# Emitting the output product of finished row blocks along with the sparse heads

## Chip, core and metric

The kernel runs on one core of one Trainium2 chip. The metric is the device time of one execution in microseconds (us), as a median over runs; for the kernel before it is 2643.86 us over 3 runs (2642.41 to 2647.59).

## What is computed

One layer of a hybrid attention encoder, for 2048 prompt rows and for a "sample" of 8 x 16 new rows with caches. One input projection feeds three groups of eight heads of 64 columns; each group's result is multiplied by a gate, and one output product ends the layer:

```python
def _merge(x, oa, ob, oc, p, w_out):
    g = jnp.concatenate([oa * jax.nn.silu(p['za']),      # A: causal, forget gate
                         ob * jax.nn.silu(p['zb']),      # B: 256 selected keys per row
                         oc * jax.nn.silu(p['zc'])], axis=-1)   # C: band of 9 chunks
    return x + jnp.einsum('bne,ed->bnd', g, w_out)       # 1536 -> 1024
...
y_prompt = _rmsnorm(hp, final_g)                         # same for y_sample
```

A row of the output thus needs all 24 heads of that row, and nothing of other rows.

## The kernel before

The 2048 prompt rows are 16 blocks of 128; block 16 is the sample. Products are made of float16 halves, so one logical product is three matmuls.

**Dense heads (A and C).** `attn_a` and `attn_c` return units of work, one for a head and a chunk of 512 queries. `chain` walks through the units: the row maxima of up to `LEAD` = 2 units run ahead of the unit whose weighted sum is being made. Each step of `chain` is emitted at high priority (`first`).

**Sparse heads (B).** `b_units` gives 32 units, two for each block of rows (four heads each), in the order of `ORDER`, block 15 first, block 0 last. A unit of block i has i + 1 steps, 272 steps in all. A step multiplies queries and keys into a `st` tile (three matmuls of 512 columns: with `KaB`, `K1B` and the mask `ng`), takes the exponential on ACT (`Pf`), its remainder `Pl` on POOL or DVE (L250), and adds twelve matmuls of 64 or 65 columns into `o` with `VB`. The maxima read `s` tiles (DVE, `jk`, L1236). A unit ends with `rs`, `u` (DVE, L1267 and L1269), `u` times the gate (POOL, L1270) and `gh` (ACT and DVE, L1272). After the second unit of a block SP issues a transposing transfer `gb<-gh` (L1275) and two writes `gTd<-gb` (L1277) into the scratch tensor `gTd` in HBM.

**The sample** (`sample_stream`, tiles `pj`, `acc`, `yy`, `rl`, `qi`) is spread over the steps 560 to 850 of `chain`, also at high priority; it writes block 16 of `gTd` (`gTd<-yy`).

**Output product.** `out_product` comes after all of this in the code. It opens the pool `ob` in the space of the dense heads' pool `aw`, loads and splits the weights `wo` (12 tiles of 128 x 1024), and for each block, `[16] + ORDER`, reads `gac<-gTd` (two transfers of 384 KB, one for each half), makes 2 x 36 matmuls of 512 columns into `pj`, adds the input row block `xr`, and normalises it: DVE L1402, ACT L1407, some 20 short DVE instructions, DVE L1413, then `out<-xr` on SP.

**What sets the order.** The code only sets priorities: a list scheduler places each engine's instructions by a timing model of its own, at high priority those of `chain` and of the sample, and fills in the others where it sees an engine free. On the chip each engine takes its list in that order.

Of the kernel before, what the change touches and what calls it, by code (L numbers as in the profile page):

```python
# [56 lines left out]
NV = 400  # L57
PITCH = 16 * 2 * NV - 1
# [4 lines left out]
def hybrid_step(ctx, tc, x_prompt, x_sample, cache_a_k, cache_a_v, cache_a_logf, cache_b_k, cache_b_v,  # L63
# [13 lines left out]
    def turn_t(out, in_):  # L77
        """blocks of 128 columns, transposed"""
        SP.dma_start_transpose(out.rearrange("p (j t) -> p j t", t=128), in_)
# [23 lines left out]
    # scratch  # L103
# [27 lines left out]
    # constants  # L131
# [110 lines left out]
    def exp_split(pool, st, lo, hi, bias):  # L242
        """P = exp: the upper halves of its words, and the rest"""
        Pf = pool.tile([128, 512], F32, name="Pf", bufs=PB)
        Pl = pool.tile([128, 512], F16, name="Pl", bufs=PB)
        Ph = Pf.bitcast(BF16).rearrange("p (n t) -> p n t", t=2)[:, :, 1]
        S.activation(Pf[:, lo:hi], st[:, lo:hi], AF.Exp, bias=bias, scale=1.0 / LOGIT)  # L247
        turn[0] += 1
        e = G if turn[0] % PD < (PN if nsl is None else PS) else V
        e.tensor_tensor(Pl[:, lo:hi], Pf[:, lo:hi], Ph[:, lo:hi], ALU.subtract)  # L250
        return Ph, Pl
# [19 lines left out]
    def finish(pool, O, hg, c):  # L271
        """gate one head of one chunk and lay it out for the output product"""
# [16 lines left out]
    def twice(e, r0, t0, n):  # L289
        """64 rows of queries, for both halves of the partitions"""  # L290
        a = qTd[e, r0:r0 + 64, t0:t0 + n]
        return bass.AP(tensor=a.tensor, offset=a.offset, ap=[[0, 2], [NT, 64], [1, n]])
# [9 lines left out]
    def vec(hh, f, off, ap):  # L302
        """rows of a table, each one element behind the row before"""
        base = rep[0, hh, f]
        return bass.AP(tensor=base.tensor, offset=base.offset + off, ap=ap)
# [5 lines left out]
    # normalised input, transposed and split  # L311
# [44 lines left out]
    def proj_t(wt, o, c, out):  # L356
        """out[col, token] for 128 columns at o"""
# [6 lines left out]
    def proj_n(wt, o, n, c, r, out, first):  # L364
        """out[token, col] for n columns at o of token block r of chunk c"""
# [90 lines left out]
    # the first chunks are projected while the next ones are normalised: forget gate, indexer, first keys and values  # L456
# [36 lines left out]
    # log sigmoid: min(x, 0) - 2 atanh((1 - T) / (3 + T)),  T = tanh(|x| / 2)  # L493
# [29 lines left out]
    # cumulative sum  # L523
# [36 lines left out]
    # position tables  # L560
# [25 lines left out]
    # indexer scores and the selected keys of one block of queries  # L586
# [25 lines left out]
    def select(i, out):  # L612
        """the 256 best keys of each row, ties to the lowest index: a threshold that 248..256 scores
        exceed, then the rest in order of value and index"""
# [49 lines left out]
        # a score equal to the threshold counts by half: take it off  # L664
# [35 lines left out]
    def select_plain(i, sl):  # L700
        """the same by 32 rounds of the eight largest"""
# [25 lines left out]
    def attn_a(h):  # L727
        """units of one head: the maxima of a chunk of queries, then its products"""
# [60 lines left out]
    def attn_c(h):  # L789
        """units of one head: the maxima of a chunk of queries, then its products"""  # L790
# [98 lines left out]
    # ------------------------------------------------------------------ the sample  # L889
    def sample_stream():  # L890
# [38 lines left out]
        def diag(t, outer):  # L929
            """the blocks on the diagonal of 8 x 8 blocks of 16 columns"""  # L930
# [116 lines left out]
        def gate_sums():  # L1047
            """forget-gate sums of the streams, relative to the end of the cache"""
# [107 lines left out]
    # ------------------------------------------------------------------ the selected keys  # L1156
    def b_units(kvp):
# [26 lines left out]
        def load_pair(c2):  # L1184
            """queries of two blocks"""
# [24 lines left out]
        def b1(u, x):  # L1210
            """the maxima of four heads"""
# [70 lines left out]
    # ------------------------------------------------------------------ order of the work  # L1282
# [7 lines left out]
    def chain(units):  # L1290
        """the maxima of the units, ahead of their products by LEAD units at most"""
        products = []
        done, k = 0, 0
        m = p = None
        while done < len(units):
            if m is None and k < len(units) and k <= done + LEAD:
                yield k
                x = []
                m = units[k][0](units[k][2], x)
                k += 1  # L1300
# [5 lines left out]
            if p is not None and next(p, END) is END:  # L1306
                p = None
                done += 1
            yield None

    def select_stream():
        """the scores of a block along with the selection of the block before"""
# [52 lines left out]
    def find_flag():  # L1365
        """rows whose threshold was not found"""
# [7 lines left out]
    def fill():  # L1374
        """projections, spread over the attention"""
# [4 lines left out]
    # ------------------------------------------------------------------ output product  # L1380
    def out_product():
        ob, ob_end = pool("ob", 2)
        wo = ob.tile([128, 2, 12, D], F16, name="wo", bufs=1)
        for k in range(12):
# [4 lines left out]
        fg = ob.tile([128, D], F32, name="fg", bufs=1)  # L1389
        SP.dma_start(fg, bass.AP(tensor=final_g.tensor, offset=final_g.offset, ap=[[0, 128], [1, D]]))  # L1390
        for b in [16] + ORDER:
            gac = ob.tile([128, 2, 12, 128], F16, name="gac")
            for e in range(2):
                SP.dma_start(gac[:, e], gTd[e, :, b * 128:(b + 1) * 128].rearrange("(k p) t -> p k t", p=128))
            xt = ob.tile([128, D], F32, name="xr")
            SP.dma_start(xt, xp[b * 128:(b + 1) * 128] if b < 16 else xs)
            for n in range(2):
                p = pj()
                seq = [(k, e, w) for k in range(12) for e, w in ((0, 0), (0, 1), (1, 0))]
                for q, (k, e, w) in enumerate(seq):  # L1400
                    mm(p, gac[:, e, k, :], wo[:, w, k, n * 512:(n + 1) * 512], start=q == 0, stop=q == len(seq) - 1)
                V.scalar_tensor_tensor(xt[:, n * 512:(n + 1) * 512], p, 1.0 / (HS * WS),  # L1402
                                       xt[:, n * 512:(n + 1) * 512], op0=ALU.mult, op1=ALU.add)
            ss = ob.tile([128, 2], F32, name="ss")
            for n in range(2):
                jk = ob.tile([128, 512], BF16, name="jk", bufs=1)
                S.activation(jk, xt[:, n * 512:(n + 1) * 512], AF.Square, accum_out=ss[:, n:n + 1])  # L1407
            ms = ob.tile([128, 1], F32, name="ms")
            V.tensor_tensor(ms, ss[:, 0:1], ss[:, 1:2], ALU.add)
            V.tensor_scalar(ms, ms, 1.0 / D, EPS, op0=ALU.mult, op1=ALU.add)  # L1410
            rr = ob.tile([128, 1], F32, name="rr")
            rsq(rr, ms, 1, ob, 1.0)
            V.scalar_tensor_tensor(xt, xt, rr, fg, op0=ALU.mult, op1=ALU.mult)  # L1413
            SP.dma_start(yp[b * 128:(b + 1) * 128] if b < 16 else ys, xt)
        ob_end.close()
# [5 lines left out]
    it = chain(units)  # L1421
# [7 lines left out]
    assert len(units) > na  # L1429
    while nsm is not None:  # L1430
        nsm += 1
        if first(smp_st) is END:
            nsm = None
    aw_end.close()
    out_product()
# [3 lines left out]
    # if a threshold was not found  # L1439
    with tc.If(fv > FORCE):  # L1440
# [4 lines left out]
        for _ in chain(b_units(None)):  # L1445
            pass
        out_product()
# [67 lines left out]
```

## Time and profile before

| | |
|---|---|
| median of 3 runs | 2643.86 us |
| span of the profiled execution | 2656.7 us |
| PE busy (matmuls) | 2393.3 us, 90% |
| DVE busy | 1866.7 us, 70% |
| ACT busy | 1368.9 us, 52% |
| POOL busy | 961.9 us, 36% |
| SP's hardware queue, share of 16 DMA engines | 40.1% |

The span runs from the first to the last instruction of the profiled execution; its own time outside the profiler is not given, and the span lies 12.8 us (0.5%) above the median of the runs. The busy time of an engine is averaged over all stages; the end of a matmul is modelled in the profile, so short waits of PE are under-counted.

### The profile page before, as it was taken

The numbers are of one execution on the slowest core, as the hardware profiler recorded it, in microseconds if no ns is written. First come the engines' busy times: TensorE is split into PE (matmuls) and PEld (weight loads), VectorE is DVE, ScalarE is ACT, GpSimd is POOL, SyncE is SP. The second block draws the span as 40 slices with busy tenths as digits, with TensorE's granted clock in tenths as the row PEclk, the third lists the DMA queues.
The fourth block names the chain that finished last, engine by engine and source line by source line (L and its number), as shares of the span: only waits on it lengthen the run. The fifth ranks groups of instructions, "written<-read, shape, count | busy, mean of one in ns | idle before, by whom it ended". The sixth has DMA issues, their size and how long they took to land.

```text
span 2656.7 us, 69205 instructions
## 1 busy us (share of the span) xinstructions
PE 2393.3 (90%) x26566; PEld 1654.3 (62%) x26566; DVE 1866.7 (70%) x5128; ACT 1368.9 (52%) x2725; POOL 961.9 (36%) x2241
## 2 busy tenths in 40 slices
PE   3898899999989989889999898879889999999998
PEld 2576567676766757666767666656656656555443
DVE  4334675877667766677677777888999988677433
ACT  5334464665547456465657465567666545433100
POOL 0013654344245243334333324535444454333000
PEclk9999999999999999999999999989999999999999
DMA  9747223343342323233333231664463322344542
GB/s 225 151 108 204 70 67 77 95 104 89 93 102 72 86 72 87 69 86 91 95 87 93 76 98 48 150 142 108 119 163 84 79 47 50 76 102 103 138 118 83
DMA packets 589286, 266.15 MB, mean 100 GB/s; under 512 B 412160, under 2 KB 577856, under 8 KB 588688
## 3 DMA queue, kind: packets, MB, share of 16 engines
q1 hardware_dynamic: 588944, 261.63, 40.1%
q8 instruction: 210, 3.44, 0.6%
q14 instruction: 132, 1.08, 0.1%
HBM read 160.37 MB, written 84.85 MB: 92 GB/s over the span
## 4 chain that ended last, share of the span: by engine, by line
PE 44%; DVE 16%; POOL 13%; DMA 11%; issue 9%; ACT 6%; SPq 1%; ACTq 0%; DVEq 0%; POOLq 0%
PE pj L72 27%; PE st L72 7%; PE o L72 4%; PE s L72 4%; ACT eq L637 2%; DMA wst<-in_w_in 2%; DVE jk L1236 2%; DVE Pl L250 2%; POOL ub L646 2%; DVE mx L759 1%; POOL eb L648 1%; DVE acc L607 1%; POOL eg L653 1%; DMA hT<-xh 1%; DMA rl<-out 1%
## 5 line engine op out<-in xcount | busy, mean ns | idle before, releaser
L72 PE MATMUL pj<-wt,hT 128*128 128x128 f16 (+1 forms) x8568 | 821.9, 244 | 2.0 <-DVE ev L82 1.0
L72 PEld LDWEIGHTS <-hT 128*128 128x128 f16 x8976 | 673.5, 99 | 210.9 <-DMA hT<-xh 50.6
L250 POOL TENSOR_TENSOR Pl<-Pf 128x512 f16<-128x512 f32 (+3 forms) x331 | 345.4, 1052 | 548.9 <-ACT Pf L247 473.6
L247 ACT ACTIVATE Pf<-st,sh 128x512 f32<-128x512 f32 (+1 forms) x496 | 295.4, 613 | 278.1 <-PE st L72 80.9
L72 PEld LDWEIGHTS <-Pf 128*128 128x128 bf16 x5472 | 326.1, 98 | 104.3 <-ACT Pf L247 20.5
L250 DVE TENSOR_TENSOR Pl<-Pf 128x512 f16<-128x512 f32 (+3 forms) x485 | 290.8, 606 | 102.7 <-ACT Pf L247 98.5
L72 PE MATMUL pj<-hT,wt 128*128 128x512 f16 (+1 forms) x1680 | 353.2, 355 | 1.2 <-DVE ev L82 1.0
L72 PEld LDWEIGHTS <-Pl 128*128 128x128 f16 x2736 | 258.8, 99 | 85.6 <-POOL Pl L250 30.4
L72 PE MATMUL pj<-wo,gac 128*128 128x512 f16 x1224 | 273.2, 380 | 3.4 <-DMA gac<-gTd 3.4
L72 PE MATMUL o<-V,Pf 128*128 128x65 f16 x3296 | 257.6, 195 | 13.8 <-ACT Pf L247 12.5
L637 ACT ACTIVATE eq<-acc,u 128x384 bf16<-128x384 f32 (+13 forms) x126 | 164.8, 1308 | 162.7 <-POOL u L660 159.1
L607 DVE SCALAR_TENSOR_TENSOR acc<-rl,iws,acc 128x512 f32<-128x512 f32 (+3 forms) x266 | 185.4, 697 | 89.8 <-ACT rl L601 86.6
L72 PEld LDWEIGHTS <-wt 128*128 128x128 f16 x1680 | 150.3, 99 | 148.6 <-issue 19.2
L72 PE MATMUL o<-V,Pl 128*128 128x65 f16 x1648 | 213.7, 194 | 29.0 <-POOL Pl L250 17.6
L247 ACT ACTIVATE Pf<-st,ncb 128x512 f32<-128x512 f32 (+1 forms) x320 | 191.3, 621 | 89.3 <-PE st L72 58.5
L1236 DVE CUSTOM_DVE_ANT_0 jk<-s,ng 128x512 bf16<-128x512 f32 (+3 forms) x304 | 187.2, 616 | 41.5 <-PE s L72 21.2
L759 DVE TENSOR_REDUCE mx<-s 128x1 f32<-128x512 f32 (+3 forms) x320 | 188.7, 602 | 33.5 <-PE s L72 32.5
L72 PEld LDWEIGHTS <-gac 128*128 128x128 f16 x1224 | 117.7, 98 | 141.1 <-DMA gac<-gTd 3.9
L601 ACT ACTIVATE rl<-s 128x512 f32<-128x512 f32 (+3 forms) x304 | 160.6, 540 | 85.4 <-PE s L72 70.4
L72 PE MATMUL st<-qp,Ka 128*128 128x512 f16 (+3 forms) x544 | 176.7, 330 | 13.9 <-ACT Pf L247 13.2
L72 PE MATMUL st<-Q,K 98*128 98x512 f16 (+3 forms) x544 | 172.8, 332 | 1.8 <-ACT Q L75 1.7
L72 PE MATMUL o<-VB,Pf 128*128 128x65 f16 (+1 forms) x2176 | 159.3, 194 | 1.1 <-ACT Pf L247 1.1
(473 smaller groups left out, 4465.3 us busy)
## 6 DMA issues: line engine op xcount, KB each, us to landing
wst<-in_w_in SPq DMA_DIRECT2D x84, 256.0 KB
gac<-gTd SPq DMA_DIRECT2D x34, 384.0 KB
out<-ev SPq DMA_DIRECT2D x96, 128.0 KB
qTd<-ev SPq DMA_DIRECT2D x96, 128.0 KB
szd<-ev SPq DMA_DIRECT2D x96, 128.0 KB
qp<-qTd SPq DMA_DIRECT2D x96, 128.0 KB
out<-xr SPq DMA_DIRECT2D x17, 512.0 KB
xt<-in_x_prompt SPq DMA_DIRECT2D x16, 512.0 KB
```

Of the source, the lines that this page charges most:

```text
L72: P.matmul(out, lhsT, rhs, start=start, stop=stop, skip_group_check=True)
L247: S.activation(Pf[:, lo:hi], st[:, lo:hi], AF.Exp, bias=bias, scale=1.0 / LOGIT)
L250: e.tensor_tensor(Pl[:, lo:hi], Pf[:, lo:hi], Ph[:, lo:hi], ALU.subtract)
L601: S.activation(r[:, :w], p[:, :w], AF.Relu)
L607: V.scalar_tensor_tensor(acc[:, k0:k0 + w], r[:, :w], iws[:, i, h:h + 1], acc[:, k0:k0 + w], op0=ALU.mult, op1=ALU.add, **kw)
L637: S.activation(jk[:, :n], x, AF.Sign, bias=b, accum_out=ss)
L646: G.tensor_scalar(ub, w, ub, None, op0=ALU.max)
L648: G.tensor_scalar(eb, a, eb, None, op0=ALU.max)
L653: G.tensor_tensor(g, e, ep, ALU.mult)
L759: V.reduce_max(mx[:, ii, kc:kc + 1], p[:, :w], axis=AX.X)
L1236: V.tensor_tensor_reduce(out=jk[:, :w], in0=p[:, :w], in1=ng[:, k0:k0 + w], scale=1.0, scalar=GONE, op0=ALU.add, op1=ALU.max, accum_out=mx ...
```

## The change

The output product becomes a generator that is started inside the loop over `chain`. As soon as the products of all dense units are emitted (`ndone[0] >= na`), the rest of the sample is emitted in one go, `aw` is closed and `ob` opened. From there on each step of the loop also emits one piece (`OUTN` = 1) of the output stream: one weight tile, or six of a block's matmuls. A prompt block may start when both its sparse units are done; the sample's block 16 is still first. What is left is emitted after the loop.

```diff
+    def out_block(ob, wo, fg, b):
...
+        for n in range(2):
+            p = pj()
+            seq = [(k, e, w) for k in range(12) for e, w in ((0, 0), (0, 1), (1, 0))]
+            for q, (k, e, w) in enumerate(seq):
+                mm(p, gac[:, e, k, :], wo[:, w, k, n * 512:(n + 1) * 512], start=q == 0, stop=q == len(seq) - 1)
+                if q % 6 == 5:
+                    yield
...
+    def out_stream(ob, wo, fg, ready):
+        yield from out_weights(ob, wo)
         for b in [16] + ORDER:
...
+            while b not in ready:
+                yield None
+            yield from out_block(ob, wo, fg, b)
...
+    it = chain(units, ndone)
+    out, ready = None, {16}
     while (v := first(it)) is not END:
...
-    assert len(units) > na
-    while nsm is not None:
-        nsm += 1
-        if first(smp_st) is END:
-            nsm = None
-    aw_end.close()
-    out_product()
+        if out is None and len(units) > na and ndone[0] >= na:
+            while nsm is not None:
+                nsm += 1
+                if first(smp_st) is END:
+                    nsm = None
+            aw_end.close()
+            ob, ob_end, wo, fg = out_open()
+            out = out_stream(ob, wo, fg, ready)
+        if out is not None:
+            for k in range(max(0, ndone[0] - na) // 2):
+                ready.add(ORDER[k])
+            for _ in range(OUTN):
+                next(out, END)
+    for k in ORDER:
+        ready.add(k)
+    for _ in out:
+        pass
+    ob_end.close()
```

Every engine has the same instructions as before; only their order differs, and only from the last dense heads on.

The first place is SP's list where the sample's last rows are written to `gTd` and block 16 is read back. `ng<-negd6` and `ng<-negd10` are the masks of sparse blocks 6 and 10, loaded shortly ahead of their units. Before:

```order
L1251 DMA sz_41607<-szd_65 128x4x64
L1152 DMA gTd_66<-yy_29338 64x4x128 x2
L1394 DMA gac_43990<-gTd_66 128x12x128
L1192 DMA qp1_42282<-qTd_63 64x4x256
L1204 DMA ng_41824<-negd6_75 128x896
L1193 DMA qp1_42282<-qTd_63 64x4x256
```

And after the change:

```order
L1153 DMA gTd_66<-yy_29338 64x4x128 x2
L1404 DMA gac_36475<-gTd_66 128x12x128
L1404 DMA gac_37145<-gTd_66 128x12x128
L1404 DMA gac_36475<-gTd_66 128x12x128
L1252 DMA sz_39797<-szd_65 128x4x64
L1404 DMA gac_37145<-gTd_66 128x12x128
L1193 DMA qp1_40969<-qTd_63 64x4x256
L1205 DMA ng_40205<-negd10_79 128x1408
```

The end of the sample and the start of the output product move from the place where the mask of sparse block 6 is loaded to that of block 10; block 15 (`gac_37145`) is read at the same place.

The second place is SP's list where sparse block 8 is finished: its transposing transfer, its writes, and what follows. Before (`gac_44218` is block 14):

```order
L1251 DMA sz_41832<-szd_65 128x4x64
L1275 DMA_TRANSPOSE gb_41598<-gh_40819 128x8x128
L1277 DMA gTd_66<-gb_41598 128x4x128 x2
L1251 DMA sz_42058<-szd_65 128x4x64
L1204 DMA ng_42286<-negd5_74 128x768
L1394 DMA gac_44218<-gTd_66 128x12x128 x2
```

After (`gac_42569` is block 8 itself):

```order
L1252 DMA sz_42882<-szd_65 128x4x64
L1276 DMA_TRANSPOSE gb_42565<-gh_41672 128x8x128
L1278 DMA gTd_66<-gb_42565 128x4x128 x2
L1404 DMA gac_42569<-gTd_66 128x12x128 x2
L1425 DMA out_0<-xr_41916 128x1024
L1252 DMA sz_43158<-szd_65 128x4x64
```

The block just written is now read back at once; before, the block read there had been written long ago. Blocks 7 to 4 follow the same pattern.

The third place is PE's list where the output product of block 8 begins after the change (`VB` belongs to the sparse unit that runs then):

```order
L73 MATMUL o_42595<-VB0_30623,Pf_42757 128x64
L73 LDWEIGHTS Pl_42758
L73 MATMUL o_42595<-VB0_30623,Pl_42758 128x65
L73 LDWEIGHTS gac_42569
L73 MATMUL pj_42575<-wo_36145,gac_42569 128x512
L73 LDWEIGHTS gac_42569
L73 MATMUL pj_42741<-wo_36145,gac_42569 128x512
```

Most matmuls of sparse block 7, and all of the lower blocks, stand behind these; before the change block 8 of the output product stood behind all sparse units.

Counted over PE's list: the sample's last matmul had 194 of the 272 sparse steps ahead of it before, and 102 after; of the 1224 matmuls of the output product 414 stood ahead of the last sparse matmul before, and 1026 after. The first matmul of the output product stands 290 rows (145 matmuls) behind the sample's last before, and 136 rows (68 matmuls) after. Between the last product of a block's second sparse unit and the first matmul of its output product stand, for blocks 8, 7, 6, 5 and 4, now 115, 123, 128, 96 and 152 matmuls, of which 16, 6, 37, 20 and 0 belong to the output product of other blocks; blocks 15 to 9 and 3 to 0 have more.

## Rows read from the trace of the kernel before

**Rows 1.** The page: the span, and busy time of the engines.

```profile
span 2656.7 us, 69205 instructions
...
PE 2393.3 (90%) x26566; PEld 1654.3 (62%) x26566; DVE 1866.7 (70%) x5128; ACT 1368.9 (52%) x2725; POOL 961.9 (36%) x2241
```

**Rows 2.** Busy time by stretch; the first numbers are the stretch and its length.

```profile
core 0: us, PE busy (x) PEld busy (x) DVE busy (x) ACT busy (x) POOL busy (x), PEclk, DMA share, GB/s
1690.00:1895.00 205.00, 170.03 (x2418) 121.58 (x2416) 179.19 (x483) 140.46 (x319) 99.36 (x108) 0.96 0.55 127
...
1942.00:2081.00 139.00, 127.96 (x1744) 85.81 (x1745) 131.66 (x385) 90.58 (x193) 64.22 (x64) 1.00 0.46 109
2081.00:2272.00 191.00, 180.53 (x2431) 120.98 (x2430) 169.09 (x506) 95.93 (x169) 95.94 (x102) 0.99 0.25 56
...
2281.00:2469.00 188.00, 187.04 (x1693) 102.26 (x1694) 135.24 (x439) 68.54 (x121) 59.12 (x61) 0.99 0.45 100
2469.00:2644.00 175.00, 174.95 (x815) 79.11 (x811) 65.43 (x268) 16.31 (x45) 0.73 (x1) 1.00 0.43 115
2644.00:2656.70 12.70, 0.00 (x0) 0.00 (x0) 5.15 (x23) 0.72 (x2) 0.00 (x0) 0.59 0.12 46
```

**Rows 3.** The chain that ended last, from 2268 to 2290: start, duration, what.

```profile
2271.16 3.71 DMA yy<-acc
...
2274.88 2.15 DMA gTd<-yy
...
2277.05 4.20 DMA gac<-gTd
...
2285.92 0.52 PE o L72 x17
```

**Rows 4.** PE's groups in 1942:2081, 2081:2272 and, last two, 2281:2469.

```profile
L72 PE MATMUL st<-Q2b,K1B 98*128 98x512 f16 x73 | 27.8, 380 | 0.0
...
L72 PE MATMUL st<-Q2b,K1B 98*128 98x512 f16 x103 | 39.2, 381 | 0.0
...
L72 PE MATMUL pj<-wo,gac 128*128 128x512 f16 x415 | 98.6, 381 | 3.4 <-DMA gac<-gTd 3.4
...
L72 PE MATMUL st<-Q2b,K1B 98*128 98x512 f16 x69 | 26.5, 384 | 0.0
```

**Rows 5.** The chain that ended last, from 1640 to the end.

```profile
1741.91 5.56 DMA rl<-in_cache_c_v
...
2469.13 174.84 PE pj L72 x810
...
2649.37 1.28 DVE xr L1413
```

**Rows 6.** PE's waits from 1690 to 2272: us, times, longest.

```profile
PE pj L968 <- ACT yy L75: 9.9, 6, 3.4
...
PE s L72 <- DVE mx L1236: 9.7, 21, 1.0
```

**Rows 7.** Timeline behind the last sparse unit's last product, and SP's part of it.

```profile
2468.90 0.10 PEld L72 LDWEIGHTS <-Pl 128*128 128x128 f16 x1
...
2469.94 0.73 POOL L1270 TENSOR_TENSOR u<-u,sz 128x256 f32<-128x256 f32 x1 [4.18 <-DVE u L1269]
...
2471.15 0.42 DVE L1272 TENSOR_TENSOR gh<-u,gh 128x256 f16<-128x256 f32 x1 [1.34 <-ACT gh L75]
2471.60 2.11 SPq L1275 DMA_TRANSPOSE gb<-gh  x1
...
2475.70 1.91 SPq L1277 DMA_DIRECT2D gTd<-gb  x2
```

**Rows 8.** Busy time by stretch around two waits of PE.

```profile
2178.80:2182.00 3.20, 0.34 (x2) 0.00 (x0) 1.22 (x4) 0.00 (x0) 1.91 (x2) 1.00 0.58 123
2182.00:2185.40 3.40, 3.28 (x39) 2.38 (x40) 3.40 (x11) 1.88 (x3) 0.00 (x0) 0.50 0.30 81
...
2281.00:2284.40 3.40, 3.11 (x17) 1.45 (x18) 1.14 (x3) 0.00 (x0) 0.00 (x0) 0.50 1.26 208
```

More of the change, by code (lines that the diff above doesn't have):

```diff
@@ L57 @@
 NV = 400
+OUTN = 1
 PITCH = 16 * 2 * NV - 1
@@ L1288, in first, with chain @@
             return next(g, END)
-    def chain(units):
+    ndone = [0]
+    def chain(units, done):
         products = []
-        done, k = 0, 0
+        k = 0
         m = p = None
-        while done < len(units):
-            if m is None and k < len(units) and k <= done + LEAD:
+        while done[0] < len(units):
+            if m is None and k < len(units) and k <= done[0] + LEAD:
                 yield k
@@ L1307, in chain @@
                 p = None
-                done += 1
+                done[0] += 1
             yield None
@@ L1378, in fill, with out_open, out_weights @@
             nfl = None if next(fil_st, END) is END else nfl + 1
-    def out_product():
+    def out_open():
         ob, ob_end = pool("ob", 2)
         wo = ob.tile([128, 2, 12, D], F16, name="wo", bufs=1)
+        fg = ob.tile([128, D], F32, name="fg", bufs=1)
+        SP.dma_start(fg, bass.AP(tensor=final_g.tensor, offset=final_g.offset, ap=[[0, 128], [1, D]]))
+        return ob, ob_end, wo, fg
+    def out_weights(ob, wo):
         for k in range(12):
@@ L1388, in out_product @@
             split_lo(wo[:, 1, k, :], wst, WS, wo[:, 0, k, :])
-        fg = ob.tile([128, D], F32, name="fg", bufs=1)
-        SP.dma_start(fg, bass.AP(tensor=final_g.tensor, offset=final_g.offset, ap=[[0, 128], [1, D]]))
-        for b in [16] + ORDER:
[L1392 to L1414, printed above, removed]
@@ L1415, in out_product @@
-        ob_end.close()
+            yield
+    def out_block(ob, wo, fg, b):
+        gac = ob.tile([128, 2, 12, 128], F16, name="gac")
+        for e in range(2):
+            SP.dma_start(gac[:, e], gTd[e, :, b * 128:(b + 1) * 128].rearrange("(k p) t -> p k t", p=128))
+        xt = ob.tile([128, D], F32, name="xr")
+        SP.dma_start(xt, xp[b * 128:(b + 1) * 128] if b < 16 else xs)
+        ss = ob.tile([128, 2], F32, name="ss")
+        for n in range(2):
[4 more added lines that the diff above has]
+                if q % 6 == 5:
+                    yield
+            xn = xt[:, n * 512:(n + 1) * 512]
+            V.scalar_tensor_tensor(xn, p, 1.0 / (HS * WS), xn, op0=ALU.mult, op1=ALU.add)
+            jk = ob.tile([128, 512], BF16, name="jk", bufs=1)
+            S.activation(jk, xn, AF.Square, accum_out=ss[:, n:n + 1])
+        ms = ob.tile([128, 1], F32, name="ms")
+        V.tensor_tensor(ms, ss[:, 0:1], ss[:, 1:2], ALU.add)
+        V.tensor_scalar(ms, ms, 1.0 / D, EPS, op0=ALU.mult, op1=ALU.add)
+        rr = ob.tile([128, 1], F32, name="rr")
+        rsq(rr, ms, 1, ob, 1.0)
+        V.scalar_tensor_tensor(xt, xt, rr, fg, op0=ALU.mult, op1=ALU.mult)
+        SP.dma_start(yp[b * 128:(b + 1) * 128] if b < 16 else ys, xt)
+        yield
@@ L1420, in hybrid_step @@
     na = len(units)
-    it = chain(units)
+    it = chain(units, ndone)
+    out, ready = None, {16}
     while (v := first(it)) is not END:
@@ L1444, in hybrid_step @@
         fb_end.close()
-        for _ in chain(b_units(None)):
+        for _ in chain(b_units(None), [0]):
             pass
-        out_product()
+        ob, ob_end, wo, fg = out_open()
+        for _ in out_stream(ob, wo, fg, set(range(NB))):
+            pass
+        ob_end.close()
         closers.pop(0).close()
```

## The prediction

> **What bounds the kernel now.** I read the page first: PE is busy 90% of the span, every other engine 70% or less [rows 1], so the question is where PE's missing tenth lies and whether the moved matmuls can get there. The table by stretch shows it. From 1690 to 1895 the dense heads and the sample run together; from 1895 to 2272 the sparse heads and the sample (I use the part from 1942, the end of the first sparse unit); from 2281 to 2469 the sparse heads and the first third of the output product; from 2469 to 2644 the output product alone [rows 2]. With the sample PE idles 35.0, 11.0 and 10.5 us in its three stretches; beside the output product it idles 1.0 of 188 us, and alone 0.05 of 175. So the output product already fills PE where it is there, and the idle time is the sample's. The last 810 matmuls take 174.84 us back to back, 216 ns each, and the normalisation of the last block ends the span 12.7 us later [rows 2, 5].
>
> Why does PE idle beside the sample? The list of waits names ACT and DVE: `yy` from ACT, and `mx`, the maxima, from DVE [rows 6]. DVE is busy 131.66 of 139 us in the denser part of the sample and 169.09 of 191 in the thinner one [rows 2].
>
> The chain of waits shows the joint between the two stretches: the sample's last transfers take 3.71, 2.15 and 4.20 us one behind the other, and PE waits for the third [rows 3], 3.4 us [rows 4].
>
> **What the change does to the sum.** It adds and removes no instruction. PE's work stays, so the time changes only by PE's idle time and its clock. There are five terms.
>
> (1) The sample gets denser. Prices first: in 2281 to 2469 PE is busy 187.0 us with 415 output matmuls, 89.6 us at 216 ns, and 69 sparse steps, hence 1.41 us a step [rows 2, 4, 5]. From 1942 to 2272 it is busy 308.5 us with 73 + 103 steps, 248 us, so the sample's part is 60 us [rows 2, 4]. After the change 102 instead of 194 steps stand ahead of the sample's end, 92 fewer; behind the first sparse unit that leaves 84 steps, 118 us, and about 56 us of the sample (92 of its some 1290 matmuls there move ahead of that unit): 174 us of PE work. How much idle time comes with it? In the thin part it is 10.5 on 180.5 us (5.8%), in the dense part 11.0 on 128.0 (8.6%), beside the dense heads 35.0 on 170.0 (20.6%) [rows 2]. The stretch after the change holds more sample work per step than any part beside the sparse heads now, and DVE is at 95% in the dense part already, so I take 8.6%: 15 us, against 21.5 now. That is **-6 us**; with 5.8% it would be -11, with 20.6% +15.
>
> The output product does not fill this idle time after the change either, and that is the point of the whole prediction: block 16 is its first block, and its matmuls stand behind the sample's last one on PE as before. The weights were loaded well ahead of use and are no matter.
>
> (2) The joint. 145 matmuls cover the wait for block 16 now, 68 after. At 74 ns each (180.53 us for 2431 [rows 2]) 10.7 us of cover become 5.0. The transfers behind them are the same, so the wait of 3.4 us [rows 4] grows to some 9; as several other matmuls of the stretch are the long ones of 216 ns, I take +4. **+4 us**, between 0 and +6.
>
> (3) The mixed stretch grows. 612 more output matmuls (132 us) move in front of the last sparse product, and with the 92 steps that come out from beside the sample this stretch gets about 437 us of PE work instead of 187, with the same six output matmuls to a step. At 1.0 idle on 187 [rows 2] that is 2.3 us: **+1 us**; with the rate of the thin sample part +24, at no idle time -1. The blocks' normalisation comes along: its DVE work is 65.43 us for the 11 blocks of the last 175 us, some 50 us for the 8.5 blocks that move, and DVE is free for 53 of 188 us there, so for some 120 of 437 [rows 2]; it hides under PE, and without that cover would cost its 50 us. SP gets the reads and writes of nine more blocks between the loads of `ng` and `qp`; also today these stand among them.
>
> (4) The output product catches up with the sparse heads. It starts while sparse block 12 runs (102 steps in) and takes a block for each block that they finish, so from block 8 on each block is read as soon as it is written. What must happen between a unit's last product and the first output matmul of its block? Behind the last unit of today `gh` is there 2.6 us after the product; `gb` is issued, and 4.1 us later the writes to `gTd` [rows 7]; a write takes 2.15 and a read 4.20 us [rows 3], and the second half of the block is issued half a microsecond behind. That is 13.6 us, in a moment when DVE has little else to do. The joint says the same: 10.7 us of cover and 3.4 us of wait. I take 14. The cover after the change is, for blocks 8, 7, 6, 5 and 4, at 74 ns for sparse matmuls and 216 ns for output ones: 10.8, 10.0, 14.7, 9.9 and 11.2 us. PE stands still for the difference, 3.2, 4.0, 0, 4.1 and 2.8 us, with everything queued behind the waiting matmul on it: the next sparse unit's products and maxima, and so ACT and DVE soon after. **+14 us**; at best nothing (the reads come 4 us sooner than I think), at worst 8 us each at four blocks, +32, if DVE is as late with `gh` as it is beside the sample.
>
> (5) The clock. Behind two waits of PE, of 3.2 us at 2179 and of 3.4 us at the joint, the granted clock is 0.50 for 3.4 us (1.2 instead of 2.4 GHz) [rows 4, 8]. That costs up to 1.7 us each. Two or three of the waits in (4) are as long: **+4 us**, between 0 and +7.
>
> The sum is -6 + 4 + 1 + 14 + 4 = +17 us on a span of 2656.7. The profiled execution lies 12.8 us over the median of the runs; I carry the difference over as it is: 2643.9 + 17 = **2661 us**, some 2674 for the span. What comes behind the last sparse product shrinks from 810 matmuls to 198, 175 to 43 us, and the last block's read is still covered by the 126 matmuls ahead of it (27 us).
>
> [...] In 2469 to 2644 weight loads are busy 79.11 of 175 us, while matmuls follow each other at 216 ns without a gap [rows 2, 5]. [...]
>
> **The rivals.** *Faster: the blocks arrive in time.* If a unit's result is back in 11 us instead of 14, terms (4) and (5) vanish, the joint costs little, and the sample's -6 to -11 is left: about 2636. It decides at the cover of blocks 8 to 4, some 10 to 11 us. For it: transfers vary, and a PE that stands still gives DVE time. Against: both chains that the trace shows need 13 to 14 us.
>
> *The sample chokes.* Packed denser, its loads of the caches could stand in the way as at 1741, where one of them alone holds up the chain for 5.56 us [rows 5]. With the idle share of 1690 to 1895, term (1) is +15 instead of -6: 2682, and up to 2705 with the thin part's rate in (3). Against: the DMA engines are busy 0.55 beside the dense heads, 0.46 and 0.25 beside the sparse ones [rows 2].
>
> *Nothing to see.* Waits of 1 to 2 us instead of 3 to 4 in (4) and the gain in (1) cancel: within 5 us of 2644.
>
> *Half of PE is free.* If moved matmuls took no time beside sparse ones, the 612 would save 132 us: 2512. In 2281 to 2469 they take their full time, since PE has no gap there [rows 2]. [...]
>
> That the change does not do what it says is ruled out by PE's list: 1026 instead of 414 output matmuls stand ahead of the last sparse one.
>
> **Chances.** The forecast 0.48, the choking sample 0.16, nothing to see 0.15, faster by arrival in time 0.19, half of PE free 0.02. A difference of 0.2% (5.3 us) is about what a measurement of this kernel can tell. So: slower 0.64, same 0.15, faster 0.21. The range for 8 in 10 reaches from 2635, the faster rival, to 2692, inside the choking one; the forecast's own, with (4) between 8 and 20 us, is 2650 to 2672.
>
> **What would show it.** In the new profile PE's waits should name `DMA gac<-gTd` about five times, 3 to 9 us each, at the joint and at blocks 8, 7, 5 and 4, with the granted clock at 0.50 behind some of them; the sample should end near 2140, with PE idle 12 to 20 us between the first sparse unit and there; behind the last sparse product some 43 us of output matmuls should be left. If PE's waits for `gac` are below 6 us in all, (4) is wrong; if the sample ends after 2165, (1) is.

## The result, and the profile after

The kernel after takes 2662.34 us, a median of 4 runs (2658.39 to 2667.73); the kernel before, beside it, 2643.14 (2642.06 to 2647.59). The ratio is 1.0070, with a 95% interval of 1.0055 to 1.0084: slower by 19 us, where +17 was forecast. The profiled execution of after is the shortest of its four, 2658.39 us, with a span of 2655.6. The profile's page of after gives the span and the busy time of each engine, and further down the output matmuls as one group:

```profile
span 2655.6 us, 69024 instructions
...
PE 2393.0 (90%) x26472; PEld 1657.1 (62%) x26566; DVE 1858.6 (70%) x5128; ACT 1368.7 (52%) x2725; POOL 961.6 (36%) x2241
...
L73 PE MATMUL pj<-wo,gac 128*128 128x512 f16 x1224 | 283.2, 379 | 8.8 <-DMA gac<-gTd 8.4
```

Every engine is about as busy as in [rows 1], so the loss is idle time. (94 of the 26566 matmuls left no record here. Where they are missing, PE's idle time reads too long, so below I go by lengths of stretches.) The list of PE's waits between the sample's end and the last sparse product names it (us, times, longest):

```profile
PE pj L73 <- DMA gac<-gTd: 8.4, 7, 2.2
PE s L73 <- DVE mx L1237: 3.0, 6, 1.1
PE tr L73 <- DVE mh L265: 1.4, 2, 1.0
PE st L73 <- ACT Pf L248: 1.1, 1, 1.1
```

The first wait is at the joint (2.2 us); the other six, 6.2 us, are at blocks 8, 7, 5 and 4, two of them for the second half of a block. The chain of waits goes through the reads of all four blocks; these are its pieces at blocks 8 and 5 (start, duration, what):

```profile
2391.88 3.05 DMA gb<-gh
2394.95 2.01 DMA gTd<-gb
2396.97 3.73 DMA gac<-gTd
2400.75 1.04 PE pj L73 x4
...
2497.09 3.06 DMA gb<-gh
2500.59 2.16 DMA gTd<-gb
2502.76 6.42 DMA gac<-gTd
2509.23 4.71 PE pj L73 x21
```

The last product of block 8 ends at 2388.5; its first output matmul starts at 2400.75, 12.2 us later. For blocks 7, 5 and 4 it is 13.9, 11.9 and 17.5 us. The forecast's 14 us was this chain.

**Reading the two profiles against each other.** Their spans differ by 1 us, the medians by 19. The two programs are the same for the first 1650 us or so, and there the profiled execution of before was already 11 us behind: one and the same DVE instruction (the 2851st, a `mx<-s` of the dense heads) begins at 1660.1 us in before and at 1649.0 in after. From there to the end it is 996.6 us before and 1006.6 after. All lengths below start at this instruction. To have typical executions of both I ran both kernels again.

### The profile page after: what moved, and what is told of

It reads as the page before. It is cut to its first block, busy times and chain, and to the rows that moved or that the text cites. A ratio compares the mean times of both kernels' runs of the same rounds, so it can differ in the third digit from the quotient of the medians.

```text
span 2655.6 us, 69024 instructions
## 1 busy us (share of the span) xinstructions
PE 2393.0 (90%) x26472; PEld 1657.1 (62%) x26566; DVE 1858.6 (70%) x5128; ACT 1368.7 (52%) x2725; POOL 961.6 (36%) x2241
## 5 line engine op out<-in xcount | busy, mean ns | idle before, releaser
L73 PEld LDWEIGHTS <-Pf 128*128 128x128 bf16 x5472 | 319.5, 98 | 112.6 <-ACT Pf L248 27.4
L73 PE MATMUL pj<-wo,gac 128*128 128x512 f16 x1224 | 283.2, 379 | 8.8 <-DMA gac<-gTd 8.4
L760 DVE TENSOR_REDUCE mx<-s 128x1 f32<-128x512 f32 (+3 forms) x320 | 188.4, 602 | 31.8 <-PE s L73 31.2
L73 PE MATMUL o<-VB,Pf 128*128 128x65 f16 (+1 forms) x2176 | 151.5, 194 | 6.3 <-ACT Pf L248 4.9
```

The costliest lines, as they stand in the source:

```text
L73: P.matmul(out, lhsT, rhs, start=start, stop=stop, skip_group_check=True)
L760: V.reduce_max(mx[:, ii, kc:kc + 1], p[:, :w], axis=AX.X)
```

## The experiments

In a table at the end of this section each kernel has three facts read from its trace: the sparse steps ahead of the sample's last matmul (of 272), the output matmuls ahead of the last sparse product (of 1224), and what it costs against the kernel before ahead of the first output matmul and behind it.

The expectations set three theories of the loss against each other. Just-in-time: PE waits for reads of blocks that were written only a moment ago. Mixing: output matmuls among the sparse heads hold these up, whenever their blocks were ready. Dense sample: the sample, squeezed beside fewer sparse steps, is what costs.

### The kernel before, and the kernel after, once more

No edit.

> The kernel before, unchanged, once more: its first profile was 11.2 us later than that of the kernel after in the part that both programs share (the DVE instruction no. 2850 begins at 1660.1 and at 1649.0 us), so the stretches of the two can't be subtracted as they stand. If that is chance of one execution, the new profile has this instruction at 1645 to 1655 us and a span of 2637 to 2646; if the program of before is slower there by itself, at 1657 to 1663. Time 2643 by either.

> The kernel after, unchanged, beside the other experiments: the kernel before took 2653.3 there, 10 us more than in the first comparison, while the kernel with the far reads took 1.0021 of it. Just-in-time theory: the change costs what it did, ratio 1.0055 to 1.0085, and so the far reads gave back 9 to 17 us of it. If the ratio is 1.004 or less, most of the loss is not in the reads. In its profile PE should again wait for gac 6 to 12 us in all between the sample's end and the last sparse product.

Before: 2652.91 us, ratio 0.9999 (0.9987 to 1.0012) to the other runs of it. The time is 10 us over what I expected by either theory. The runs from here on are from three chips, whose medians of before agree (2653.3 to 2654.6 us); which chip the first comparison ran on is not on record, so the cause of the 10 us stays open. Expectations in us below were made with 2643 for before in mind, so I compare by ratios. The instruction above begins at 1657.4 us here, which by my expectation would speak for a program that is slower there by itself; but the whole execution is longer than I had expected, after has the instruction at 1654.0, 3 us earlier and not 11, and the eleven kernels from here on have it between 1653.9 and 1658.8. So most of the 11 us between the first two profiles was chance of single executions. After: 2670.83 us, ratio 1.0069 (1.0053 to 1.0085), the same loss. Busy time by stretch, first for before and then for after, cut at the instruction above, the first sparse matmul, the sample's last matmul, the first output matmul, the last sparse product and the last output matmul:

```profile
core 0: us, PE busy (x) PEld busy (x) DVE busy (x) ACT busy (x) POOL busy (x), PEclk, DMA share, GB/s
1657.40:1858.40 201.00, 170.85 (x2354) 122.98 (x2354) 174.70 (x444) 130.91 (x296) 98.30 (x109) 0.94 0.58 134
1858.40:2263.80 405.40, 374.24 (x5088) 251.56 (x5085) 373.79 (x1088) 237.50 (x465) 189.89 (x197) 0.99 0.38 90
2263.80:2279.10 15.30, 10.62 (x144) 6.45 (x140) 8.90 (x19) 8.01 (x13) 9.18 (x10) 1.00 0.31 68
2279.10:2467.10 188.00, 187.32 (x1693) 102.26 (x1694) 133.52 (x439) 68.48 (x121) 59.27 (x61) 0.99 0.45 100
2467.10:2642.00 174.90, 174.86 (x812) 79.05 (x808) 65.33 (x268) 16.31 (x45) 0.73 (x1) 1.00 0.43 115
2642.00:2654.60 12.60, 0.00 (x0) 0.00 (x0) 5.14 (x23) 0.72 (x2) 0.00 (x0) 0.64 0.12 47
```

```profile
1654.00:1853.60 199.60, 170.75 (x2358) 123.80 (x2358) 169.61 (x447) 130.21 (x297) 93.87 (x106) 0.92 0.59 135
1853.60:2138.40 284.80, 248.30 (x3478) 174.68 (x3511) 252.85 (x746) 168.89 (x355) 122.63 (x131) 0.98 0.44 105
2138.40:2150.50 12.10, 7.37 (x67) 3.44 (x65) 10.03 (x35) 3.10 (x6) 2.96 (x4) 1.00 0.47 103
2150.50:2612.80 462.30, 447.61 (x3891) 241.68 (x3948) 299.06 (x970) 155.21 (x271) 136.06 (x136) 1.00 0.38 89
2612.80:2655.50 42.70, 42.70 (x198) 19.16 (x196) 15.93 (x60) 4.03 (x11) 0.72 (x1) 1.00 0.36 95
2655.50:2668.20 12.70, 0.01 (x1) 0.00 (x0) 5.16 (x23) 0.72 (x2) 0.00 (x0) 0.68 0.12 46
```

The work that lies behind the first output matmul is 362.2 us of PE before (187.32 + 174.86) and 491.6 after (taken from the next kernel's trace, which has the same matmuls there, all recorded), so 129.4 us moved behind it. Ahead of it, before needs 621.7 us; after should need 492.3 and needs 496.5: 4.2 us lost. Behind it, 375.5 + 129.4 = 504.9 would be even, and it is 517.7: 12.8 us lost. In the pair of the first comparison the same sums give 1.8 us won ahead and 11.8 lost behind. **The loss is behind the first output matmul, in the mixed stretch.**

### Reads that nobody has to wait for

```diff
-            SP.dma_start(gac[:, e], gTd[e, :, b * 128:(b + 1) * 128].rearrange("(k p) t -> p k t", p=128))
+            SP.dma_start(gac[:, e], gTd[e, :, SEQ:NT].rearrange("(k p) t -> p k t", p=128))
```

> As the change, but each prompt block's two reads fetch the columns of block 16 from gTd, which were written long before: the same bytes in as many transfers, no dependence on the sparse head just finished. So the outputs of the 16 prompt blocks are not the reference's. The sample part on PE is the same row for row (102 steps). Just-in-time theory: PE's waits for gac vanish (8.4 us before), and with them the waits of the sparse heads behind them; 2646 to 2655. Mixing theory and dense-sample theory: within 4 us of the change, 2658 to 2667.

2657.34 us, ratio 1.0021 (1.0012 to 1.0030): 0.0048 or 13 us less than after. As ratios to the 2643 us that I had in mind, 2646 to 2655 is 1.001 to 1.005 and 2658 to 2667 is 1.006 to 1.009, so the just-in-time theory is met and the other two are not; some 5 us of the loss are left. By stretch, and then all of PE's waits of the mixed stretch:

```profile
1653.90:1850.50 196.60, 166.36 (x2358) 120.84 (x2358) 171.16 (x447) 130.08 (x297) 93.82 (x106) 0.95 0.61 137
1850.50:2134.70 284.20, 252.31 (x3513) 175.90 (x3510) 251.51 (x746) 169.79 (x356) 122.91 (x131) 0.96 0.43 105
2134.70:2146.70 12.00, 7.43 (x67) 3.44 (x65) 9.93 (x35) 3.11 (x6) 2.94 (x4) 1.00 0.46 104
2146.70:2636.80 490.10, 489.43 (x4135) 260.61 (x4136) 316.07 (x1027) 159.13 (x281) 134.88 (x136) 1.00 0.38 91
2636.80:2639.00 2.20, 2.20 (x12) 0.78 (x8) 0.75 (x3) 0.42 (x1) 0.72 (x1) 1.00 0.03 7
```

```profile
PE pj L73 <- DMA gac<-gTd: 2.6, 1, 2.6
PE s L73 <- DVE mx L1237: 0.6, 2, 0.4
```

The one read waited for is the sample's, at the joint; that wait ends where the mixed stretch begins. Within the stretch PE idles 0.7 us on 490, though more output matmuls than ever (1214 instead of 1026: with the dependency gone the scheduler placed more of them there) stand among the sparse heads. So mixing by itself costs nothing there: the mixing theory falls. The waits for `mx`, `mh` and `Pf` that after has besides those for `gac` are gone as well: they were the echo of the waits for `gac`, in sparse units that had been held up behind them on PE. That is why 6 us of direct waits cost 12 to 13.

### Readiness one block later, and three

```diff
-            for k in range(max(0, ndone[0] - na) // 2):
+            for k in range(max(0, ndone[0] - na - 2) // 2):
...
+            for k in range(max(0, ndone[0] - na - 6) // 2):
```

> As the change, but a block counts as ready one block later. Two blocks are still read just in time: 10.6 and 9.0 us of other PE work stand ahead of blocks 6 and 5, 14.6 and 14.5 ahead of 8 and 7 (10.8, 10.9, 14.7, 10.2 and 11.4 us ahead of 8 to 4 with the change, 39 to 11 with the lag of three). The sample ends at sparse step 103 (102 with the change). Just-in-time theory, at a latency of some 13 us from the last product of a block to its first output matmul: two waits for gac of 2 to 4 us instead of four to six, so about half of what the lag of three gave back: ratio 1.001 to 1.005. If readiness is no matter, 1.0055 or more.

> As the change, but a block counts as ready three blocks later (units 7 and 8 behind its own instead of its own two), so the order by itself gives the reads time: 39, 28, 14, 11 and 26 us of other PE work ahead of the first matmul of blocks 8 to 4 (11, 11, 15, 10 and 11 with the change), with the outputs of the reference. The sample ends at sparse step 112 (102 with the change), 1032 output matmuls stand ahead of the last sparse one. Just-in-time theory: as with the far reads, within 3 us of 1.002 of the kernel before; PE's waits for gac below 5 us, the joint's among them. Mixing and dense-sample theories: as the kernel after, 1.005 to 1.0085.

One block: 2655.63, ratio 1.0006 (0.9993 to 1.0019). Three: 2649.96, ratio 0.9993 (0.9982 to 1.0004). PE's waits for `gac` are 2.4 us in both, the joint's with them (8.1 in after, in the same view); first one block later, then three:

```profile
PE pj L73 <- DMA gac<-gTd: 2.4, 3, 1.2
PE pj L73 <- DMA gac<-gTd: 2.4, 2, 1.4
```

Here the reads are the real ones, and the loss is gone too. Both are faster than I had expected (1.001 to 1.005, and 1.001 to 1.003). With one block of lag the half of the way that I expected is what one sees behind the first output matmul: there it loses 6 us instead of 13. But ahead of it, with the sample's end one sparse step later, it wins 7 where after loses 4.

### Two pieces of the output product per step

```diff
-OUTN = 1
+OUTN = 2
```

> As the change, with one number doubled: two pieces of the output product are emitted per step instead of one, by the same rule of readiness. One would think that the output product then catches up with the sparse heads earlier; on PE's list it is the other way: no block is read just in time (23 us or more of other work ahead of each, 10 ahead of block 16), the sample ends at sparse step 115 (102 with the change, 112 with the lag of three), 1044 output matmuls stand ahead of the last sparse one. Just-in-time theory: no wait for gac of a prompt block, 1 us or so at the joint; like the lag of three or a little better, ratio 0.996 to 1.000.

2649.00, ratio 0.9977 (0.9965 to 0.9988). PE waits for `gac` once, 1.2 us at the joint, and idles not at all from there to the last sparse product. One constant turns the loss into a small gain, and through the order alone.

### The early end of the sample without the mixing

```diff
         if out is not None:
             for k in range(max(0, ndone[0] - na) // 2):
                 ready.add(ORDER[k])
-            for _ in range(OUTN):
-                next(out, END)
+            pass
```

> The pool, the weights' loader and the early end of the sample as in the change, but the output product is emitted only behind the last sparse unit. On PE the sample then ends at sparse step 183 instead of 194 (102 with the change), and 524 output matmuls instead of 414 (1026) stand ahead of the last sparse one, none of them behind less than 25 us of other work. All theories: what costs in the change is the place of the output matmuls, so this is the kernel before, 2640 to 2647, with the sample's end at 2230 to 2260 us. If it is 2655 or more, the cost is in the early end of the sample's emission or in the pool, and all of them fall.

2637.07, ratio 0.9940 (0.9923 to 0.9958). I had expected no change, and it is 16 us faster than before. By stretch:

```profile
1654.40:1850.30 195.90, 170.77 (x2351) 122.39 (x2351) 174.31 (x444) 130.09 (x295) 99.26 (x109) 0.94 0.59 136
1850.30:2233.60 383.30, 356.48 (x4911) 241.42 (x4908) 354.31 (x1048) 228.30 (x452) 183.75 (x189) 1.00 0.38 93
2233.60:2248.60 15.00, 13.90 (x173) 8.29 (x169) 13.73 (x40) 8.89 (x15) 8.42 (x10) 1.00 0.48 95
2248.60:2471.80 223.20, 222.13 (x1954) 120.19 (x1955) 152.02 (x498) 77.85 (x139) 68.23 (x70) 1.00 0.42 100
2471.80:2622.90 151.10, 151.10 (x702) 68.28 (x698) 56.74 (x228) 14.14 (x39) 0.72 (x1) 1.00 0.43 114
```

All of it is won ahead of the first output matmul: 594.2 us, with 11.0 us of work moved behind it, against 621.7. PE's idle time falls in each of the three stretches there, 30.2 to 25.1, 31.2 to 26.8 and 4.7 to 1.1 us, 13 us in all; the other 3.5 us are PE's own work, 917.9 us in the rows of before and 914.4 in these, at a granted clock that is nearer to 1.00 in the second stretch. So emitting the rest of the sample at once, with 183 sparse steps still to lie beside it, goes with a gain of 16 us. The change emits it in the same way, but the mixing leaves it only 102 steps, and in far and after nothing is left of the 16 us.

The lists of PE's waits, from the common instruction to the sample's last matmul, show where: ahead of the sample's own `pj` matmuls. In before these waits come to 17 and 19 us in the two profiles, here to 8.5, in far to 20.2, in after to 18 and 21. The largest of these rows in far, and the same row here:

```profile
PE pj L969 <- DVE qi L83: 8.7, 9, 2.0
PE pj L969 <- DVE qi L83: 2.0, 3, 0.8
```

### The old pace of the sample, with the mixing

Two kernels keep the sample's old pace; the second also takes block 16 last and counts a block as ready two blocks later:

```diff
-        if out is None and len(units) > na and ndone[0] >= na:
-            while nsm is not None:
...
+        if out is None and len(units) > na and nsm is None:
```

```diff
-        for b in [16] + ORDER:
+        for b in ORDER + [16]:
...
-            while nsm is not None:
-                nsm += 1
-                if first(smp_st) is END:
-                    nsm = None
...
-            for k in range(max(0, ndone[0] - na) // 2):
+            for k in range(max(0, ndone[0] - na - 4) // 2):
```

> The output product is emitted along with the sparse heads as in the change, but only once the sample is emitted at its old pace. The sample ends at sparse step 155, 1070 output matmuls stand ahead of the last sparse one (1026 with the change), and every prompt block is read behind 17 us or more of other PE work (10 to 15 us with the change at blocks 8 to 4). Just-in-time theory: PE's waits for gac go from 8.4 to below 3 us; the time is 2640 to 2648. Mixing theory (output matmuls among the sparse heads hold these up, whenever their blocks were ready): as many are mixed in, so 2655 to 2665, with PE idle 10 us or more between the sample's end and the last sparse product. Dense-sample theory (the early sample is what costs): about halfway, 2648 to 2655, and the loss lies ahead of the sample's end.

> The one arrangement in which output matmuls can stand in the sample's idle time: the sample keeps its old pace, the output product begins when the dense heads are done with the blocks of the sparse heads (each ready two blocks later), and block 16 comes last. 107 output matmuls stand ahead of the sample's end at sparse step 155, 954 ahead of the last sparse one; 23 us or more of other work ahead of each block but 5 and 4 (12 and 11 us). No joint is left. If the sample's waits (some 60 us of PE's idle time in the kernel before) can be filled by ready work in PE's order, 107 matmuls are 23 us and a good part of that comes off: ratio 0.988 to 0.994. If the order is fixed so that a waiting sample matmul holds up the output ones as well, the gain is that of the joint alone, and the ratio is that of the kernel with the sample at its old pace, 0.996 to 0.999.

The first: 2644.53, ratio 0.9975 (0.9961 to 0.9988), PE's wait for `gac` is 3.4 us (below 3 was expected), all of it at the joint, and the rest of the mixed stretch has 0.1 us of idle time: as the just-in-time theory has it, and a little faster than before. So this kernel gains some 7 us by its ratio without the early end of the sample, and by the table ahead of the first output matmul. The second: 2650.61, ratio 0.9986 (0.9977 to 0.9995), in the range of the fixed order: no joint is left, and 107 output matmuls lie among the sample's. But they lie where PE waits little. From the first of them to the sample's end it idles 2.1 us:

```profile
2132.50:2227.80 95.30, 93.16 (x1233) 63.02 (x1245) 66.80 (x231) 37.17 (x72) 38.68 (x46) 1.00 0.27 65
```

The rest of PE's idle time up to the sample's end, some 60 us as in before, lies ahead of the first of them. So whether ready output matmuls could fill the sample's waits is not shown either way.

### The mixing begun later

```diff
-            for _ in range(OUTN):
-                next(out, END)
+            if ndone[0] >= na + 14:
+                for _ in range(OUTN):
+                    next(out, END)
```

(And the same with 8 for 14.)

> As the change, but the output product is first emitted when 14 more sparse units are done. The sample ends at sparse step 146 (102 with the change, 183 when the output product comes last), 1064 output matmuls stand ahead of the last sparse one, each block's first matmul behind 15 us or more of other work. What is open: the kernel whose sample ends at step 183 is 16 us faster than before, the far reads' with its end at step 102 is 4 us slower, with the same idle time of PE behind the sample. Theory of the sample's density: the fewer sparse steps the sample has beside it, the more of its waits PE sees, so this one lies between, ratio 0.995 to 1.000. Theory that the early flush gives the gain and the place of the output matmuls costs nothing once no read is just in time: 0.993 to 0.995, as with the output product last.

> As the change, but the output product is first emitted when 8 more sparse units are done. On PE the sample ends at sparse step 146 and 1064 output matmuls stand ahead of the last sparse one, each block's first behind 15 us or more of other work. (The kernel that waited for 14 units had, by its trace, the sample's end at step 182 and 765 output matmuls ahead of the last sparse one, not the 146 and 1064 that its expectation gave, so it told nothing between 112 and 183; these are the numbers of this one.) Density theory, the cost growing evenly as the sample is squeezed: between the lag of three (0.9993 at step 112) and 0.994 at step 183, so 0.996 to 0.998. Theory that it costs only where the sample's own chain has no slack left, below step 110 or so: 0.9925 to 0.995, as with the late starts.

With 14: 2634.41, ratio 0.9936 (0.9920 to 0.9952), the fastest of all, within the error of the sample ended early without mixing; the order in its trace (182 steps and 765 matmuls) was not the one that its expectation gave, so it repeats that kernel rather than telling anything between. With 8: 2641.57, ratio 0.9950 (0.9932 to 0.9968), which lies at the border of the two expectations and decides nothing between an even growth and a threshold; by the table most of the cost comes below 146 steps.

| kernel | sparse steps ahead of the sample's end | output matmuls ahead of the last sparse product | us ahead / behind | ratio |
|---|---|---|---|---|
| before | 194 | 414 | 0 / 0 | 1 |
| after | 102 | 1026 | +4 / +13 | 1.0069 |
| far reads | 102 | 1214 | +1 / 0 | 1.0021 |
| ready one block later | 103 | 1038 | -7 / +6 | 1.0006 |
| ready three blocks later | 112 | 1032 | -5 together | 0.9993 |
| two pieces per step | 115 | 1044 | -7 / -1 | 0.9977 |
| mixing 8 units later | 146 | 1064 | -14 / 0 | 0.9950 |
| mixing 14 units later | 182 | 765 | -20 together | 0.9936 |
| early end, no mixing | 183 | 524 | -17 / +1 | 0.9940 |
| old pace, mixing | 155 | 1070 | -11 / 0 | 0.9975 |
| old pace, block 16 last | 155 | 954 | -8 together | 0.9986 |

"Ahead" and "behind" are worked out as for after, each from its own profiled execution, "together" where matmul records are missing (for after the work is taken from far); single executions scatter by some 5 us in them, and the profiled execution of before is itself 3.7 us above its median.

## Why the prediction was right

The forecast of 2661 us and the measured 2662 agree, and the largest term, (4), is the one that the runs confirm. That they agree within 2 us is partly luck: (2) and (5) were 8 us too dear, (1) was 4 to 10 us too cheap, and within (4) two errors cancel. The 2674 us for the span are not met (2655.6): the profiled execution was the shortest of its four.

**Term (4), the just-in-time reads: right in mechanism and place, and in size by two errors that cancel.** Blocks 8, 7, 5 and 4 wait and block 6 doesn't, as its cover said. The latency of 14 us was 12 to 17. The direct waits are 6.2 us instead of 14, none over 1.8 us for a block's first half where 3 to 9 us were forecast. There are two reasons. At blocks 8 and 5 the latency was 12.2 and 11.9 us instead of 14, with a cover as forecast (12.2 less 1.5 of wait is 10.7). At blocks 7 and 4 PE took longer over the cover than its matmuls alone: 12.4 us lay ahead of the wait instead of 10.0, and 16.4 instead of 11.2. The rest of the cost came in the waits of the held-up sparse units, which the forecast names but gives no price. By the far reads the whole is 13 us by the medians, and 12.5 by the stretch behind the first output matmul.

**Term (3), the mixed stretch: right.** I took +1 with a bound of +24. With the far reads the stretch has 0.7 us of idle time, so beyond the echo in (4) it costs nothing. The 437 us of work were a slip in the sum: 92 steps at 1.41 us are 130 us, not the 118 of the 84 steps that stay, which makes 449. The far reads' 489.4 us, less their 188 further output matmuls at 216 ns, are the same 449.

**Term (5), the clock: wrong.** I took +4; it is 0. Behind three of the waits of the profile after (the joint, blocks 8 and 5) the granted clock stays at 1.00, which is 2.4 GHz:

```profile
2138.70:2142.10 3.40, 3.38 (x29) 1.81 (x30) 1.40 (x4) 1.08 (x2) 1.16 (x2) 1.00 1.35 217
2400.70:2404.10 3.40, 3.35 (x31) 1.79 (x32) 2.38 (x14) 1.14 (x2) 1.43 (x2) 1.00 0.32 55
2506.10:2509.50 3.40, 2.54 (x23) 1.46 (x24) 2.50 (x12) 0.00 (x0) 0.00 (x0) 1.00 0.90 157
```

Once more (2670.83 us) it was 0.65 behind the joint, as it had been 0.67 before, and 1.00 behind blocks 8, 7 and 5. The step that failed is the one that took a wait of 3 to 4 us at each block for given; they were shorter, and the two waits of [rows 4, 8] from which I took the clock's drop had been 3.2 and 3.4 us. Nor would waits of that length have brought it each time, as the last section shows.

**Terms (1) and (2), the sample and the joint: -2 together, measured -2 and +4.** The joint is no worse than before (12.1 instead of 15.3 us, and PE idles 4.7 us in both), so (2) is 0, not +4: the 67 matmuls between took 7.4 us, 110 ns each and not 74. For (1), the rows from where the prediction began, the end of the first sparse unit, to the sample's end, first of before and then of the far reads, where every matmul is recorded:

```profile
1942.20:2266.00 323.80, 303.38 (x4114) 203.56 (x4111) 294.64 (x876) 182.48 (x354) 154.85 (x160) 0.99 0.35 80
1933.80:2134.70 200.90, 183.16 (x2529) 127.91 (x2529) 175.82 (x533) 113.05 (x234) 84.39 (x93) 0.95 0.38 90
```

PE idles 17.7 us on 183.2 of work (9.7%, where I took 8.6% of 174) against 20.4 in before. (At 20.6% the forecast's sum gives +14, not the +15 that it states.) That is inside the 12 to 20 us forecast, and the sample ends at 2127, near the 2140. So (1) is -3 there and not -6, and between -2 and +4 with what comes ahead of that unit, to which the prediction gave no term (-2 by the first pair of profiles, +4 by the second, +1 by the far reads).

What I had not seen is that (1) hides two things: with 183 steps beside it the sample's early end goes with a gain of 16 us, and with 102 steps nothing of that is left. That the squeezing takes it back is argued, not shown by a run that changes it alone: PE's waits ahead of the sample's own matmuls grow from 8.5 to 20 us, and from 183 to 102 steps the ratios in the table rise, but before (194 steps) and the two kernels with the old pace (155) lie off that line.

**The rivals.** "The blocks arrive in time" is what lag of three blocks and two pieces per step make of the kernel, and at ratios of 0.9993 (with 1 in its interval) and 0.9977 they are even with before and 6 us faster, where that rival was to be 8. "The sample chokes" holds in part: the sample is hardly slower than before, but the gain it could have brought is used up. "Half of PE is free": the Trainium skill, in "Perfetto Trace Analysis", section "Identifying the Most-Contended Engine", would judge TensorE's headroom by MFU (the matmuls' rate as a share of the peak) and by the busy share of LDWEIGHTS. I did not work out MFU. LDWEIGHTS is busy 260.61 of 490.10 us in the mixed stretch of the far reads; there matmuls leave 0.7 us free, and the 800 output matmuls that stand there more than before took their full time. By the trace the share of LDWEIGHTS, taken alone, does not give the headroom of this kernel.

On the chain of three transfers the Trainium skill, in "SBUF — State Buffer", section "The DMA setup-cost knee", gives a fixed cost of about 2 us to each. The write to `gTd` agrees (2.01 and 2.16 us); the transposition ahead of it and the read behind it took 3.05 and 3.73 to 6.42 us, so an estimate of 6 us by that fixed cost alone would have been too short by 3 to 6; the page adds a term for the bytes, which this estimate leaves out.

## What to carry to other kernels

When a consumer is moved next to its producer, count the work that lies between them on the engine that will wait, and compare it with the latency of the whole round trip (here 12 to 17 us through HBM, against 10 to 11 us of matmuls at the blocks that waited most): what helped here was a lag in the order; a faster transfer was not tried. A wait can cost more than its length when the instructions queued behind it feed the other engines; here 6 us of waits cost 12 to 13. And take a change that does two things apart: here the early end alone was 16 us faster than before, the mixing alone, begun behind the sample at its old pace, 7 us faster, and both together 18 us slower.

## What the runs showed that I had not expected

The granted clock behind a wait of PE is not told by the length of the wait. Behind 3.5 us at the joint of before, once more, it was 0.67 over the next 3.4 us; the third row shows why: it fell to 0.50 (1.2 GHz) only 1.2 us behind the wait's end, and then stayed there for 3.4 us. Behind 3.4 us at the joint of the kernel with the old pace and the mixing it stayed at 1.00. Behind 2.6 us in the kernel with the mixing begun 8 units later it was 0.50 at once, for 3.4 us again:

```profile
2275.50:2279.10 3.60, 0.16 (x1) 0.00 (x0) 0.00 (x0) 0.69 (x1) 2.40 (x3) 1.00 0.91 202
2279.10:2282.50 3.40, 3.38 (x20) 1.54 (x21) 1.42 (x6) 0.61 (x1) 0.00 (x0) 0.67 1.30 214
2280.27:2283.68 3.41, 3.41 (x16) 1.32 (x13) 2.52 (x8) 0.69 (x1) 0.73 (x1) 0.50 1.35 213
```

```profile
2208.70:2212.20 3.50, 0.14 (x2) 0.01 (x1) 2.26 (x8) 0.35 (x1) 0.17 (x1) 1.00 1.12 221
2212.20:2215.60 3.40, 3.35 (x37) 1.94 (x38) 1.68 (x6) 0.59 (x1) 0.00 (x0) 1.00 1.09 225
```

```profile
2194.90:2197.80 2.90, 0.32 (x5) 0.01 (x1) 1.55 (x7) 0.00 (x0) 0.00 (x0) 1.00 1.11 227
2197.80:2201.20 3.40, 3.37 (x18) 1.57 (x18) 0.73 (x5) 0.00 (x0) 0.00 (x0) 0.50 1.27 204
```

And the same kernel before has a median of 2643.1 us in the first comparison and of 2653.3 to 2654.6 in the others, while the ratio of after to before is 1.0070 and 1.0069: of a change this small, only the ratio to a run beside it can be read.
